# Delta rule's preparation: masks inside the clamp, products read from PSUM, two clamps on ScalarE

## The chip, the cores and the metric

One Trainium2 chip, one core. The metric is the device time of one execution in microseconds (us). Five engines work at once, each with its own queue in order: TensorE (PE, with its weight loads PEld), VectorE (DVE), ScalarE (ACT), GpSimd (POOL) and SyncE (SP), whose queue issues the DMAs here. SBUF is the on-chip memory, PSUM the memory that matrix products are written to.

## The reference

Two layers over 256 context tokens and 256 latent tokens, 1024 channels, in float32. A layer is a SwiGLU half step, a mix of three token mixers on one input, and another half step. The mixer that the change touches is the gated delta rule, 4 heads of 128 channels, forwards and backwards in time. Per chunk it solves a triangular system (cut; `incl` includes the diagonal, `strict` doesn't):

```
diff  = gc[..., :, None] - gc[..., None, :]
a_mat = einsum(kc, kc) * where(strict, exp(where(strict, diff, 0)), 0) * bc[..., :, None]
sol   = triangular_solve(eye(CHUNK) + a_mat, rhs, left_side=True, lower=True)
p_mat = einsum(qc, kc) * where(incl, exp(where(incl, diff, 0)), 0)
```

gc is the running sum of the log decays, bc the write strength. The other two mixers (retention, state-space) and the projections fill the time around it.

## The kernel before

All work is in float32; the large projections are made as three fast products each, so every weight block (128x512, one DMA of 256 KB, tile raw) is split into a high half by a cast on ScalarE (whi, L121) and a low half by a subtraction on VectorE or GpSimd (wlo, L123), and multiplied by L141, L142 and L143. Blocks are four buffers deep: a load waits until the casts have freed its buffer, a cast until TensorE has used the old half. 1313 such loads go through SyncE's queue, together with all other DMAs.

The function `gdn` computes the delta rule for a group of heads: heads 0 and 1, then 2 and 3 in layer 0; all four in layer 1. It projects and convolves (L533, L536), transposes (gtr), computes small columns (col), and then comes the preparation, L887 to L937, which the change is in. Chunks have 128 tokens here. For each pair of heads p, rows of running sums (Rg) and of strengths (Rb) are loaded as broadcasts; for each of four chunks c a body runs:

- L905: clamped differences on VectorE into six places of E: forward, two heads (min with 0), backward (min with 0; only where the chunk has output), and backward for the system (max with 0)
- L908, L909: exponentials on ScalarE, L909 with the sign turned
- L912, L915: products of keys with keys and with queries on TensorE, into one PSUM bank (kk, a pool of three banks, `mx`)
- L917: VectorE masks the first two into kks (strict upper triangle)
- L920, L921: the matrices M of both directions, from kks, a column and E
- L923: GpSimd multiplies M by the rows Rb
- L928: queries' products from PSUM times a column times a triangular mask into kq; L930: kq times E into PT (only where the chunk has output)
- `self.take(wt[2])`: TensorE gets other work to fill the time ("fill": projections and the retention mixer in `retention`, later the state-space projections)

In layer 0 all four chunks have output, in layer 1 only chunks 2 and 3. After the chunks L936 and L937 make Q from Rg and the queries.

Behind it SyncE's queue writes the diagonal 32x32 blocks of M to DRAM (d<-M, four writes), reads them back with another layout (B, L952), and VectorE substitutes in 31 steps (L957, L959, tiles tm and X). Then blocks are merged by products (tile XX) and the chunks are scanned.

The fill in these stretches includes the retention mixer (products rsc, L653; times a table into pt, L657 and L660, on VectorE; normalised output `on`, L680, and its transposes rof, L686) and the state-space mixer's projections (BC, transposes str, L1181; gates zs from products sz). The mixer itself has a clamp on ScalarE, L1281, followed by exponentials.

The framework orders each engine's queue at build time from priorities and estimated times, so the order in the queues isn't the order in the source.

Of the kernel before, what the change touches and what calls it, by code (L numbers as in the profile page):

```python
# [8 lines left out]
F32 = mybir.dt.float32  # L9
F32R = mybir.dt.float32r  # L10
I32 = mybir.dt.int32
AF = mybir.ActivationFunctionType
ALU = mybir.AluOpType
MUL, ADD, SUB, MAX, MIN = ALU.mult, ALU.add, ALU.subtract, ALU.max, ALU.min

P = 128
# [30 lines left out]
class Net:  # L47
# [410 lines left out]

    def mix_setup(self, ctx):
        nc, io, cp = self.nc, self.io, self.cp  # L460
        self.masks = cp.tile([P, 3, P], F32, name="masks")
        nc.sync.dma_start(out=self.masks, in_=io["masks"])
        self.triU, self.triL, self.triUs = (self.masks[:, i, :] for i in range(3))
        self.prow = cp.tile([P, DEPTH, PR_N], F32, name="prow")
        nc.sync.dma_start(out=self.prow, in_=io["prow"].rearrange("(o l) n -> o l n", o=1).broadcast_to([P, DEPTH, PR_N]))
        self.rt = cp.tile([P, 4, 48], F32, name="rt_")
        nc.gpsimd.memset(self.rt, 0.0)

        for lo, hi in ((PC_GCW, PC_GNG), (PC_GNG, PC_N)):
            v = self.pcol[:, :, lo:hi]  # L470
            nc.vector.tensor_scalar(out=v, in0=v, scalar1=0.5, scalar2=None, op0=MUL)
# [309 lines left out]
    def gdn(self, H, gp, pool0, gtok):  # L781
# [3 lines left out]
        nc, l, tc = self.nc, self.l, self.tc  # L785
        outs, och = self.outs, self.och
        nh, h0, n0 = len(H), H[0], och[0]
        nu, no = 2 * nh, len(och)
        wt = self.gdn_fill
        tag = f"{l}{h0}"  # L790
# [49 lines left out]
        for i, h in enumerate(H):  # L840
            ps = self.win_tile(OFF_GK + h * P, [0, 1], "gk")
# [3 lines left out]
            ps = self.win_tile(OFF_GQ + h * P, outs, "gq")  # L845
# [3 lines left out]
        for i, h in enumerate(H):  # L849
            ps = self.win_tile(OFF_GV + h * P, [0, 1], "gv")  # L850
# [13 lines left out]
        rk, rq, bb, w0, w1, nb0, nb1, tmp = (col[:, i] for i in range(8))  # L864
# [19 lines left out]
        M = gp.tile([P, 4, nu, P], F32, tag="M", name="M")  # L884
        PT = gp.tile([P, no, nu, P], F32, tag="PT", name="PT")
        Q = gp.tile([P, 2, nh, self.no], F32, tag="Q", name="Q")
        with ExitStack() as st:  # L887
            pp = st.enter_context(tc.tile_pool(name=f"gprep{tag}", bufs=1, side="right", reuse_waits="tile"))
            for p in range(0, nh, 2):
                Rg = pp.tile([P, 2, 2, T], F32, tag="Rg", name="Rg")  # L890
                Rb = pp.tile([P, 2, 2, T], F32, tag="Rb", name="Rb")
                for d in range(2):
                    self.rows_in(Rg[:, d], self.dR[d * 20 + h0 + p:d * 20 + h0 + p + 2, :])
                    self.rows_in(Rb[:, d], dB[d * nh + p:d * nh + p + 2, :])
                pair = lambda t, c: t[:, c].rearrange("p (d h) n -> p d h n", d=2)[:, :, p:p + 2]
                for c in range(4):
                    out = c in och
                    cs = ac(c)
                    E = pp.tile([P, 6, P], F32, tag="E", name="E", bufs=2)
                    for i in range(2):  # L900
                        for d, slot, op in ((0, i, MIN), (1, 2 + i, MIN), (1, 4 + i, MAX)):
                            if slot in (2, 3) and not out:
                                continue
                            g = h0 + p + i
                            nc.vector.tensor_scalar(out=E[:, slot], in0=Rg[:, d, i, cs], scalar1=self.G[:, c, d, g:g + 1],  # L905
                                                    scalar2=0.0, op0=SUB, op1=op)
                    ne = 4 if out else 2
                    nc.scalar.activation(out=fl(E[:, 0:ne]), in_=fl(E[:, 0:ne]), func=AF.Exp)  # L908
                    nc.scalar.activation(out=fl(E[:, 4:6]), in_=fl(E[:, 4:6]), func=AF.Exp, scale=-1.0)  # L909
                    ps = v4(self.mx("kk"))  # L910
                    for i in range(2):
                        nc.tensor.matmul(ps[:, i], kf[:, p + i, cs], kf[:, p + i, cs], start=True, stop=True)  # L912
                    if out:
                        for i in range(2):
                            nc.tensor.matmul(ps[:, 2 + i], kf[:, p + i, cs], qf[:, p + i, qc(c)], start=True, stop=True)  # L915
                    kks = pp.tile([P, 2, P], F32, tag="kks", name="kks", bufs=2)
                    nc.vector.tensor_tensor(out=kks, in0=ps[:, 0:2], in1=self.triUs.unsqueeze(1).to_broadcast([P, 2, P]), op=MUL)  # L917
                    for i in range(2):
                        q = p + i
                        nc.vector.scalar_tensor_tensor(out=M[:, c, q], in0=kks[:, i], scalar=rk[:, c, q:q + 1], in1=E[:, i], op0=MUL, op1=MUL)  # L920
                        nc.vector.scalar_tensor_tensor(out=M[:, c, nh + q], in0=kks[:, i], scalar=bb[:, c, q:q + 1], in1=E[:, 4 + i],  # L921
                                                       op0=MUL, op1=MUL)
                    nc.gpsimd.tensor_tensor(out=pair(M, c), in0=pair(M, c), in1=Rb[:, :, :, cs], op=MUL)  # L923
                    if out:
                        kq = pp.tile([P, 4, P], F32, tag="kq", name="kq", bufs=1)
                        for i in range(2):
                            for d, m in ((0, self.triU), (1, self.triL)):
                                nc.vector.scalar_tensor_tensor(out=kq[:, 2 * d + i], in0=ps[:, 2 + i], scalar=rk[:, c, p + i:p + i + 1],  # L928
                                                               in1=m, op0=MUL, op1=MUL)
                        nc.vector.tensor_tensor(out=pair(PT, c - n0), in0=kq.rearrange("p (d h) n -> p d h n", d=2),  # L930
                                                in1=E[:, 0:4].rearrange("p (d h) n -> p d h n", d=2), op=MUL)
                    self.take(wt[2])
                for d in range(2):
                    for i in range(2):
                        q_ = Q[:, d, p + i]
                        nc.scalar.activation(out=q_, in_=Rg[:, d, i, self.oc], func=AF.Exp)  # L936
                        nc.gpsimd.tensor_tensor(out=q_, in0=q_, in1=qf[:, p + i], op=MUL)  # L937
# [8 lines left out]
        with ExitStack() as st:  # L946
            pp = st.enter_context(tc.tile_pool(name=f"gsub{tag}", bufs=1, side="right", reuse_waits="tile"))
            n = 4 * nb
# [5 lines left out]
            for s in range(31):  # L954
# [3 lines left out]
                                        in1=X[:, s, 0:b].unsqueeze(1).to_broadcast([n, a, b]), op=MUL)  # L958
# [23 lines left out]
        with ExitStack() as st:  # L982
            pp = st.enter_context(tc.tile_pool(name=f"gmrg{tag}", bufs=1, side="right", reuse_waits="tile"))
# [738 lines left out]
def constants():  # L1722

    i, j = np.arange(P)[:, None], np.arange(P)[None, :]
    m = np.zeros((P, 3, P), np.float32)
    m[:, 0] = i <= j
    m[:, 1] = i >= j
    m[:, 2] = i < j
    d = np.arange(384)[None, :] - P - np.arange(P)[:, None]
    dist = d.astype(np.float32)  # L1730
    n_freq = P // 4
    inv = (np.float32(10000.0) ** (-np.arange(n_freq, dtype=np.float32) / np.float32(n_freq))).astype(np.float32)
    tok = np.arange(NS)
    ang = np.concatenate([(tok // 64).astype(np.float32)[:, None] * inv, (tok % 64).astype(np.float32)[:, None] * inv], -1).T
    cos, sin = np.cos(ang).astype(np.float32), np.sin(ang).astype(np.float32)
    rope = np.stack([np.concatenate([cos, cos]), np.concatenate([-sin, sin])], 1)
    return {"ident": np.eye(P, dtype=np.float32), "masks": m, "dist": dist, "rope": np.ascontiguousarray(rope),
            "eye32": np.eye(32, dtype=np.float32)}
# [65 lines left out]
```

## Time and profile before

| | |
|---|---|
| median of 3 runs | 2776.03 us (2774.65 to 2779.43) |
| the profiled execution | 2773.71 us, of which the span 2771.9 us |
| TensorE busy | 94% of the span |
| VectorE busy | 75% |
| ScalarE busy | 44% |
| GpSimd busy | 27% |
| granted clock of TensorE, mean | 0.978 of full speed |

Busy time is that of instructions in work. A matmul's end is modelled, so a busy TensorE need not be at its peak. A wait names the instruction that was released last.

### The profile page before, as it was taken

Reading aid. Unit: us, or ns where it says so; the run is one execution under the profiler, and the core shown is the slowest. Engines: PE = TensorE matmul, PEld = TensorE weight load, DVE = VectorE, ACT = ScalarE, POOL = GpSimd, SP = SyncE. Lnnn points to the kernel's source line nnn. Section 1 sums busy time; section 2 is a strip of 40 time slices with the busy share of each in tenths; the row PEclk is TensorE's granted clock in tenths of the full one; section 3 lists DMA queues with packets and bytes.
Section 4 is the critical chain, followed back from the end, with each engine's and each line's share of the span. In section 5 each row is a group of like instructions: output and inputs, shape, how many; then the busy total and the mean of one; then the engine's idle time right before and its main releaser. Section 6 shows DMA issues by size and latency. Waiting matters only on the chain.

```text
span 2771.9 us, 45529 instructions
## 1 busy us (share of the span) xinstructions
PE 2602.5 (94%) x16136; PEld 2216.4 (80%) x16136; DVE 2088.3 (75%) x4122; ACT 1213.0 (44%) x2388; POOL 745.7 (27%) x627
## 2 busy tenths in 40 slices
PE   8999999899899999999999999999988889889998
PEld 6888887777777777888887888888877768778997
DVE  5888878868878585488987778854778885786666
ACT  3333256344345643363332543323655354554553
POOL 1000144422444454250000520002443433453100
PEclk9999999999999999999999999999999999999999
DMA  8566655423425455366665466643545333656665
GB/s 280 178 187 188 172 165 147 118 62 105 147 77 158 155 152 156 106 172 197 194 187 185 136 208 195 189 125 97 174 115 166 110 99 89 194 184 187 199 183 152
DMA packets 292808, 435.99 MB, mean 157 GB/s; under 512 B 42628, under 2 KB 109828, under 8 KB 292452
## 3 DMA queue, kind: packets, MB, share of 16 engines
q1 hardware_dynamic: 292580, 433.09, 53.1%
q8 instruction: 126, 2.06, 0.3%
q14 instruction: 102, 0.84, 0.1%
HBM read 401.86 MB, written 31.13 MB: 156 GB/s over the span
## 4 chain that ended last, share of the span: by engine, by line
PE 63%; DVE 19%; DMA 7%; issue 5%; ACT 3%; POOL 3%; SPq 1%; DVEq 0%; ACTq 0%; POOLq 0%
PE p L141 9%; PE p L143 9%; PE p L142 9%; DVE cacc L533 4%; DMA raw<-wst 4%; PE pd L141 3%; PE pd L143 3%; PE pd L142 3%; DVE wlo L123 3%; PE gate L141 1%; PE gate L143 1%; PE gate L142 1%; ACT whi L121 1%; PE br L141 1%; PE br L143 1%
## 5 line engine op out<-in xcount | busy, mean ns | idle before, releaser
L121 ACT CAST whi<-raw 128x512 fp32r<-128x512 f32 x1003 | 613.5, 617 | 819.5 <-PE pd L142 195.4
L123 DVE TENSOR_TENSOR wlo<-raw,whi 128x512 fp32r<-128x512 f32 x803 | 596.8, 746 | 233.3 <-ACT whi L121 226.5
L141 PE MATMUL p<-uh,whi 128*128 128x512 f32 (+1 forms) x1216 | 445.3, 366 | 1.8 <-ACT whi L121 1.8
L143 PE MATMUL p<-uh,wlo 128*128 128x512 f32 (+1 forms) x1216 | 440.2, 362 | 0.2 <-DVE wlo L123 0.2
L142 PE MATMUL p<-ul,whi 128*128 128x512 f32 (+1 forms) x1216 | 440.2, 362 | 0.0
L123 POOL TENSOR_TENSOR wlo<-raw,whi 128x512 fp32r<-128x512 f32 x200 | 288.5, 1445 | 484.5 <-ACT whi L121 467.6
L190 DVE SCALAR_TENSOR_TENSOR acc<-raw,cT,acc 128x512 f32<-128x512 f32 x448 | 320.5, 753 | 87.9 <-DMA raw<-wst 86.2
L307 POOL TENSOR_TENSOR y<-y,piv 128x256 f32<-128x256 f32 x30 | 27.6, 950 | 884.5 <-ACT piv L305 884.5
L141 PEld LDWEIGHTS p<-uh,whi 128*128 128x128 f32 x1216 | 229.0, 188 | 43.4 <-ACT whi L121 4.4
L143 PEld LDWEIGHTS p<-uh,wlo 128*128 128x128 f32 x1216 | 229.1, 188 | 37.3 <-DVE wlo L123 0.6
L142 PEld LDWEIGHTS p<-ul,whi 128*128 128x128 f32 x1216 | 229.2, 188 | 34.2
L141 PE MATMUL pd<-ach,whi 128*128 128x512 f32 (+1 forms) x660 | 232.0, 351 | 0.0
L143 PE MATMUL pd<-ach,wlo 128*128 128x512 f32 (+1 forms) x660 | 229.4, 348 | 0.0
L142 PE MATMUL pd<-acl,whi 128*128 128x512 f32 (+1 forms) x660 | 229.2, 347 | 0.0
L533 DVE SCALAR_TENSOR_TENSOR cacc<-craw,pcol,cacc 128x508 f32<-128x508 f32 (+2 forms) x192 | 169.4, 889 | 17.6 <-ACT cacc L528 16.0
L141 PEld LDWEIGHTS pd<-ach,whi 128*128 128x128 f32 x660 | 125.0, 189 | 17.4 <-ACT whi L121 1.4
L143 PEld LDWEIGHTS pd<-ach,wlo 128*128 128x128 f32 x660 | 125.0, 189 | 16.3 <-DVE wlo L123 0.5
L142 PEld LDWEIGHTS pd<-acl,whi 128*128 128x128 f32 x660 | 125.0, 189 | 15.2
L141 PE MATMUL gate<-uh,whi 128*128 128x512 f32 (+1 forms) x384 | 135.4, 353 | 0.0
L143 PE MATMUL gate<-uh,wlo 128*128 128x512 f32 (+1 forms) x384 | 130.9, 341 | 0.8 <-POOL wlo L123 0.8
L142 PE MATMUL gate<-ul,whi 128*128 128x512 f32 (+1 forms) x384 | 131.4, 342 | 0.0
L411 ACT CAST ach<-pr 128x512 fp32r<-128x512 f32 (+1 forms) x88 | 50.0, 568 | 164.8 <-DVE pr L410 164.8
(477 smaller groups left out, 6057.4 us busy)
## 6 DMA issues: line engine op xcount, KB each, us to landing
raw<-wst SPq DMA_DIRECT2D x1313, 256.0 KB, 2.8
R<-dR SPq DMA_DIRECT2D x24, 512.0 KB, 6.0
dah<-y SPq DMA_DIRECT2D x9, 1024.0 KB, 5.6
y<-dah SPq DMA_DIRECT2D x28, 256.0 KB, 5.1
Rg<-dR SPq DMA_DIRECT2D x8, 512.0 KB, 5.2
Rb<-dB SPq DMA_DIRECT2D x8, 512.0 KB, 4.6
dx<-xo SPq DMA_DIRECT2D x16, 256.0 KB, 2.9
xt<-dx SPq DMA_DIRECT2D x4, 1024.0 KB, 8.4
```

The costliest lines, as they stand in the source:

```text
L121: nc.scalar.copy(out=hi, in_=r)
L123: e.tensor_tensor(out=lo, in0=r, in1=hi.bitcast(F32), op=SUB)
L141: nc.tensor.matmul(out, wh, xh, start=start, stop=False)
L142: nc.tensor.matmul(out, wh, xl, start=False, stop=False)
L143: nc.tensor.matmul(out, wl, xh, start=False, stop=stop)
L190: eng.scalar_tensor_tensor(out=acc, in0=r, scalar=c, in1=acc, op0=MUL, op1=ADD)
L307: (nc.gpsimd if m >= self.ln_dve[0] else nc.vector).tensor_tensor(out=y[:, m, c], in0=y[:, m, c], in1=piv, op=SUB)
L411: nc.scalar.copy(out=F["ach"][:, m], in_=pr[:, :n])
L533: nc.vector.scalar_tensor_tensor(out=a[:, :, lo:hi], in0=r[:, :, lo + d:hi + d], scalar=w[:, tap:tap + 1], in1=a[:, :, lo:hi], op0=MUL, op ...
```

## The change

The mask tile gets four parts instead of three: the two triangles with their diagonals, and two with 0 inside the triangle and -30000 outside. The clamp of the forward and backward places becomes one instruction that subtracts and takes the minimum with such a mask, so that the exponential is 0 outside the triangle. The third clamp (backward, for the system) goes to ScalarE as Relu with a negated column as bias; the negated columns nG are made once per pair of heads. M and PT are computed straight from the products in PSUM; kks and kq and their instructions go. M's lower triangle and diagonal, which nothing reads, are no longer zeroed.

```
-        self.masks = cp.tile([P, 3, P], F32, name="masks")
+        self.masks = cp.tile([P, 4, P], F32, name="masks")
-        self.triU, self.triL, self.triUs = (self.masks[:, i, :] for i in range(3))
+        self.triU, self.triL, self.minU, self.minL = (self.masks[:, i, :] for i in range(4))
...
+                nG = pp.tile([P, 4, 2], F32, tag="nG", name="nG", bufs=2)
+                nc.vector.tensor_scalar(out=nG, in0=self.G[:, :, 1, h0 + p:h0 + p + 2], scalar1=-1.0, scalar2=None, op0=MUL)
...
                     for i in range(2):
-                        for d, slot, op in ((0, i, MIN), (1, 2 + i, MIN), (1, 4 + i, MAX)):
-                            if slot in (2, 3) and not out:
-                                continue
-                            g = h0 + p + i
-                            nc.vector.tensor_scalar(out=E[:, slot], in0=Rg[:, d, i, cs], scalar1=self.G[:, c, d, g:g + 1],
-                                                    scalar2=0.0, op0=SUB, op1=op)
+                        g = h0 + p + i
+                        for d, low in ((0, self.minU), (1, self.minL)):
+                            if d == 0 or out:
+                                nc.vector.scalar_tensor_tensor(out=E[:, 2 * d + i], in0=Rg[:, d, i, cs], scalar=self.G[:, c, d, g:g + 1],
+                                                               in1=low, op0=SUB, op1=MIN)
+                        nc.scalar.activation(out=E[:, 4 + i], in_=Rg[:, 1, i, cs], func=AF.Relu, bias=nG[:, c, i:i + 1])
...
-                    kks = pp.tile([P, 2, P], F32, tag="kks", name="kks", bufs=2)
-                    nc.vector.tensor_tensor(out=kks, in0=ps[:, 0:2], in1=self.triUs.unsqueeze(1).to_broadcast([P, 2, P]), op=MUL)
...
-                        nc.vector.scalar_tensor_tensor(out=M[:, c, q], in0=kks[:, i], scalar=rk[:, c, q:q + 1], in1=E[:, i], op0=MUL, op1=MUL)
-                        nc.vector.scalar_tensor_tensor(out=M[:, c, nh + q], in0=kks[:, i], scalar=bb[:, c, q:q + 1], in1=E[:, 4 + i],
+                        nc.vector.scalar_tensor_tensor(out=M[:, c, q], in0=ps[:, i], scalar=rk[:, c, q:q + 1], in1=E[:, i], op0=MUL, op1=MUL)
+                        nc.vector.scalar_tensor_tensor(out=M[:, c, nh + q], in0=ps[:, i], scalar=bb[:, c, q:q + 1], in1=E[:, 4 + i],
                                                        op0=MUL, op1=MUL)
...
-                        kq = pp.tile([P, 4, P], F32, tag="kq", name="kq", bufs=1)
                         for i in range(2):
-                            for d, m in ((0, self.triU), (1, self.triL)):
-                                nc.vector.scalar_tensor_tensor(out=kq[:, 2 * d + i], in0=ps[:, 2 + i], scalar=rk[:, c, p + i:p + i + 1],
-                                                               in1=m, op0=MUL, op1=MUL)
-                        nc.vector.tensor_tensor(out=pair(PT, c - n0), in0=kq.rearrange("p (d h) n -> p d h n", d=2),
-                                                in1=E[:, 0:4].rearrange("p (d h) n -> p d h n", d=2), op=MUL)
+                            for d in range(2):
+                                nc.vector.scalar_tensor_tensor(out=PT[:, c - n0, d * nh + p + i], in0=ps[:, 2 + i], scalar=rk[:, c, p + i:p + i + 1],
+                                                               in1=E[:, 2 * d + i], op0=MUL, op1=MUL)
...
-    m[:, 2] = i < j
+    m[:, 2:] = (m[:, :2] - 1) * np.float32(30000.0)
```

## Rows read from the trace of the kernel before

**Rows 1.** The page: busy us, share of the span and instructions of each engine.

```profile
PE 2602.5 (94%) x16136; PEld 2216.4 (80%) x16136; DVE 2088.3 (75%) x4122; ACT 1213.0 (44%) x2388; POOL 745.7 (27%) x627
```

**Rows 2.** Windows, three preparations: length, busy PE, PEld, DVE, ACT, POOL; clock, DMA.

```profile
487.00:532.00 45.00, 43.35 (x202) 34.88 (x201) 36.17 (x79) 19.16 (x39) 25.87 (x24) 1.00 0.58 155
690.00:736.00 46.00, 44.74 (x211) 37.11 (x210) 36.14 (x82) 19.65 (x37) 26.67 (x23) 1.00 0.64 181
2103.00:2173.00 70.00, 57.72 (x349) 50.11 (x347) 68.53 (x182) 33.55 (x75) 30.83 (x26) 0.95 0.48 152
```

**Rows 3.** Waits of PE, 480 to 545: total us, times, longest.

```profile
PE rsc L653 <- DVE pt L657: 6.7, 1, 6.7
...
PE rg L143 <- DVE wlo L123: 1.5, 1, 1.5
```

**Rows 4.** Waits of PE, 685 to 760.

```profile
PE str L1181 <- DVE BC L536: 7.0, 1, 7.0
PE sz L143 <- POOL wlo L123: 1.3, 1, 1.3
```

**Rows 5.** Waits of PE, 2096 to 2175.

```profile
PE rsc L653 <- DVE pt L660: 5.2, 3, 4.0
PE rof L686 <- DVE on L680: 4.7, 2, 2.5
PE rq L141 <- ACT whi L121: 1.2, 1, 1.2
```

**Rows 6.** Groups of DVE, whole span: count | busy us, mean ns | idle before.

```profile
L905 DVE TENSOR_SCALAR E<-Rg,G 128x128 f32<-128x128 f32 x88 | 33.2, 426 | 5.2 <-DMA Rg<-dR 5.2
L920 DVE SCALAR_TENSOR_TENSOR M<-kks,col,E 128x128 f32<-128x128 f32 x32 | 17.1, 543 | 0.1
L921 DVE SCALAR_TENSOR_TENSOR M<-kks,col,E 128x128 f32<-128x128 f32 x32 | 15.3, 488 | 0.0
L928 DVE SCALAR_TENSOR_TENSOR kq<-kk,col,masks 128x128 f32<-128x128 f32 x48 | 14.2, 339 | 0.0
L930 DVE TENSOR_TENSOR PT<-kq,E 128x512 f32<-128x512 f32 x12 | 13.2, 1098 | 0.0
L917 DVE TENSOR_TENSOR kks<-kk,masks 128x256 f32<-128x256 f32 x16 | 6.6, 414 | 0.7 <-PE kk L915 0.7
```

**Rows 7.** Instructions by tile (E; kq): count: ns shortest/median/longest, first and last start.

```profile
L1281 ACT ACTIVATE E<-R,G x192: 383/388/405, 872.8 to 2479.1; 128x128 f32<-128x128 f32 x192
L905 DVE TENSOR_SCALAR E<-Rg,G x88: 271/277/1382, 488.2 to 2166.2; 128x128 f32<-128x128 f32 x88
L920 DVE SCALAR_TENSOR_TENSOR M<-kks,col,E x32: 335/346/1397, 496.7 to 2168.5; 128x128 f32<-128x128 f32 x32
L930 DVE TENSOR_TENSOR PT<-kq,E x12: 677/684/1796, 499.8 to 2170.8; 128x512 f32<-128x512 f32 x12
L928 DVE SCALAR_TENSOR_TENSOR kq<-kk,col,masks x48: 331/339/347, 489.7 to 2170.2; 128x128 f32<-128x128 f32 x48
```

**Rows 8.** Timeline of DVE: start, us, instruction.

```profile
702.36 1.37 DVE L920 SCALAR_TENSOR_TENSOR M<-kks,col,E 128x128 f32<-128x128 f32 x1
...
707.54 1.11 DVE L928 SCALAR_TENSOR_TENSOR kq<-kk,col,masks 128x128 f32<-128x128 f32 x4
```

**Rows 9.** Timeline of POOL; in brackets the idle time before and its releaser.

```profile
701.83 3.04 POOL L937 TENSOR_TENSOR Q<-Q,qf 128x512 f32<-128x512 f32 x2 [2.24 <-ACT Q L936]
```

**Rows 10.** Waits of ACT, 480 to 545.

```profile
ACT E L908 <- DVE E L905: 14.6, 4, 4.5
```

**Rows 11.** Products kk of PE, 480 to 530.

```profile
L912 PE MATMUL kk<-kf x16: 270/275/275, 486.8 to 505.6; 128*128 128x128 f32 x16
```

**Rows 12.** Timeline of SyncE's queue, 476 to 545.

```profile
518.31 0.34 SPq L945 DMA_DIRECT2D d<-M  x1
...
523.75 0.34 SPq L110 DMA_DIRECT2D raw<-wst  x1
524.14 0.42 SPq L945 DMA_DIRECT2D d<-M  x1
```

More of the change, by code (lines that the diff above doesn't have):

```diff
@@ L1724, in constants @@
     i, j = np.arange(P)[:, None], np.arange(P)[None, :]
-    m = np.zeros((P, 3, P), np.float32)
+    m = np.zeros((P, 4, P), np.float32)
     m[:, 0] = i <= j
     m[:, 1] = i >= j
-    m[:, 2] = i < j
+    m[:, 2:] = (m[:, :2] - 1) * np.float32(30000.0)
     d = np.arange(384)[None, :] - P - np.arange(P)[:, None]
```

## The prediction

> **What bounds the kernel now.** First the busy shares of the whole execution: TensorE is busy for 94% of 2771.9 us, VectorE for 75%, ScalarE for 44%, GpSimd for 27% [rows 1]. TensorE's work doesn't change here, apart from waits. So the question is how much of its idle time hangs on the delta rule's preparation.
>
> The preparation runs three times: heads 0 and 1 of layer 0, heads 2 and 3 of layer 0, all four heads of layer 1. I cut one window per run, from the first product of keys to the start of the substitution or the last PT [rows 2]. In the first two, TensorE is busy for 43.35 of 45 and 44.74 of 46 us while VectorE has 36 us of work; in the third VectorE is busy for 68.53 of 70 us and TensorE for only 57.72. There VectorE is the bound, and TensorE's 12.3 idle us are the price.
>
> Then who holds TensorE up, in windows stretched to the waits that the preparation causes further on. Layer 0, first run: 6.7 us in one piece for the retention table product (the tile pt) behind VectorE's queue, and 1.5 us for a weight's low half on VectorE [rows 3]. Second run: 7.0 us for BC and 1.3 us for a low half on GpSimd [rows 4]. Layer 1: 5.2 us for pt and 4.7 us for the normalised retention output on VectorE, besides 1.2 us for a weight cast [rows 5]. The ceiling of what these stages can give back is 8.2 + 8.3 + 12.3 = 28.8 us.
>
> **The change part by part.** There are 16 bodies (a pair of heads, one chunk of 128 tokens): 12 with output, 4 without (chunks 0 and 1 of layer 1, two pairs).
>
> *VectorE before.* 88 clamps, 16 maskings into kks, 64 products for M, 48 for kq and 12 for PT: 228 instructions, 99.6 us by the six groups [rows 6]. Two things are in that sum. One is plain length: 0.277 us a clamp, 0.346 a product from SBUF, 0.339 a product from PSUM, 0.684 a PT [rows 7], 0.414 a kks [rows 6]. In a row they start closer than they last: four kq products take 1.11 us together [rows 8], so they start (1.11 - 0.34) / 3 = 0.26 us apart, and each instruction occupies the engine for about 0.08 us less than its length. The other is stalls: M products that read two SBUF tensors take 1.37 us, four times in a row from 702.36 on [rows 8], while GpSimd works on Q without a break [rows 9]. Clamps and PT show it too (maxima 1.38 and 1.80), but the 48 products that read PSUM and a mask never do: 331 to 347 ns [rows 7]. So on this trace a VectorE instruction is held up by GpSimd when it reads two SBUF tensors or is a clamp, and not when one operand is in PSUM.
>
> By starts, mean lengths times counts less 0.08 us each: 37.5 + 6.6 + 17.4 + 15.6 + 16.3 + 13.2 - 228 x 0.08 = 88 us occupied. Without stalls it would be 88 x 0.20 + 16 x 0.33 + 64 x 0.26 + 48 x 0.26 + 12 x 0.60 = 59 us.
>
> *VectorE after.* 56 clamps with a mask (4 in each of 12 bodies, 2 in each of 4), 64 M products from PSUM, 48 PT products from PSUM: 168 instructions at 0.26 = 44 us. The clamps now read Rg and a mask, two SBUF tensors, so I give them the mean stall of the old M products: (17.4 + 15.6) / 64 - 0.346 = 0.17 us, times 56 = 9.5 us. M and PT get none, after kq. The four small instructions for nG I take as whole clamps, 1 us. Sum 54.5 us, so 33 to 34 us less VectorE time; 34 below. Bounds: 14 us, if every stall moves to a neighbour (59 - 45), and 43 us, if the clamps escape it (88 - 45). I take 34, as the trace has both kinds of product side by side.
>
> [...]
>
> *ScalarE.* 32 clamps move there as Relu with a column as bias. The state-space stage runs exactly that form at 0.388 us [rows 7]: 12.4 us. ScalarE is busy for 19.16 of 45, 19.65 of 46 and 33.55 of 70 us [rows 2], so about 0.8 us more in each body finds room. What covers it is idleness in front of the exponentials: in the first run they wait 14.6 us for VectorE's clamps [rows 10], and those now have fewer ahead of them. Queued behind a Relu are the weight casts that TensorE lives on; if the cover were gone, the 12.4 us would be the price. No exchange of function tables is charged: Relu and Exp already alternate there.
>
> *Removed tiles, and a wait.* kks and kq go. The product's bank is now read only after the exponential, so it is held longer. The pool has three such banks, and TensorE's next products queue behind a held one. In the first run the products are issued from 486.8 to 505.6 us [rows 11], some 6 us apart, so a bank has three such steps to come free. I charge nothing; without that slack it would be up to one 6 us step per run. M's diagonal and lower part are no longer zeroed; nobody's instruction count hangs on it. The mask load grows from 192 to 256 KB and is made once, early, on a queue of 1313 weight loads of that size: nothing.
>
> *What reaches the end.* GpSimd finishes M, SyncE's queue writes its diagonal blocks to DRAM and reads them back, and VectorE substitutes. In the first run the queue hangs at the first write until 518.31; the fourth leaves at 524.14, behind a weight load at 523.75 [rows 12], and the read back later still. Weight loads wait until casts free their buffers, and those follow TensorE. So an M that is ready 10 us earlier does not move the read back by 10 us: once the queue is no longer held up by M, it is held by weights. I take the 1.5 us for the low half and 1 us of the 6.7: **2.5 us**, between 0 and 8.2. In the second run GpSimd, not weights, trails M, so I take 3 of the 7.0 us and 1 of the 1.3: **4 us**, between 0 and 8.3. In layer 1 the queue in front of pt and the retention output loses its share of the 34 us (100 of 228 instructions, 15 us of 68.5), which should pay about half of TensorE's idle time: **6 us**, between 0 and 12.3. Sum 12.5 us. What is late next is the weight stream and, after the substitution, DMA; neither is touched.
>
> **The rivals.**
> 1. *The queue gives nothing away.* The preparation gets faster, but the read back stays behind weight loads, and the time is lost as a longer wait for DRAM. For it: the weight load ahead of the last write [rows 12]. Against it: layer 1's waits for pt and on are in the same VectorE queue, with no DRAM between. Then 0 to 5 us come back: 2771 to 2776.
> 2. *The whole ceiling.* The order of the queues, which is chosen at build time, moves with the shorter preparation, and nearly all 28.8 us return. For it: all long waits name VectorE. Against it: the queue of [rows 12]. Some 20 to 29 us: 2747 to 2756.
> 3. *Slower: ScalarE blocks the weights.* A Relu must wait for the row load and for E's buffer (two of them, freed by VectorE), and the casts behind it on ScalarE stand. TensorE pays as now at a late cast, 1.2 us [rows 5], once a body: 16 x 1.2 = 19, less the 12.5 gained: 7 us slower, 2783. It decides once a Relu stands longer than the casts are ahead; today's waits of the exponentials, 14.6 us over four bodies, some 4 us each [rows 10], cost TensorE nothing in that run.
>
> **How the numbers follow.** The profiled execution took 2773.71 us (span 2771.9); 2773.7 - 12.5 = 2761.2. The median of the runs shown is 2776.03, 2.3 us more, so 2763.5. Chances: forecast, 6 to 20 us gained, 0.48; rival 1 (within 5.5 us of the old time) 0.23; rival 2, 0.14; rival 3 and any other loss, 0.15. A measurement of this kernel can tell about 0.2%, 5.5 us, from no change. So faster 0.62, same 0.23, slower 0.15. The range leaves out the best of rival 2 and the worse part of rival 3: 2749 to 2779; the forecast's own is 2756 to 2770.
>
> **What would show it right or wrong.** In the profile after: M and PT products reading PSUM at 0.34 us with no maximum above 0.4; masked clamps near 0.35 with maxima near 1.4; 32 more Relu at 0.39; the groups of [rows 6] shrunk from 99.6 to some 65 us busy (168 x 0.34 + 9.5); TensorE's waits for pt and on in layer 1 about halved; the 6.7 us of [rows 3] hardly shorter. Wrong would be: M products slow from PSUM, waits of TensorE for weight casts in these windows, or TensorE standing at a product kk.

## The result and the profile after

Seven runs of the changed kernel have a median of 2762.19 us (2758.49 to 2771.60), seven of the kernel before beside them 2777.51 us (2767.07 to 2786.65): ratio 0.9949, interval [0.9929, 0.9970], some 14 us faster; 12.5 us were forecast. The profiled execution took 2766.53 us (span 2764.7). The seven executions of one kernel spread over 13 us (changed) and 20 us (before), so gains below are read in the stages, not from two spans.

Groups of VectorE after; columns as in [rows 6]:

```profile
L907 DVE SCALAR_TENSOR_TENSOR E<-Rg,G,masks 128x128 f32<-128x128 f32 x56 | 39.5, 751 | 2.4 <-DMA Rg<-dR 2.4
L929 DVE SCALAR_TENSOR_TENSOR PT<-kk,col,E 128x128 f32<-128x128 f32 x48 | 13.5, 340 | 0.0
L922 DVE SCALAR_TENSOR_TENSOR M<-kk,col,E 128x128 f32<-128x128 f32 x32 | 10.9, 342 | 2.7 <-ACT E L911 2.0 <-PE kk L918 0.7
L923 DVE SCALAR_TENSOR_TENSOR M<-kk,col,E 128x128 f32<-128x128 f32 x32 | 10.9, 341 | 1.9 <-ACT E L912 1.9
L897 DVE TENSOR_SCALAR nG<-G 128x8 f32<-128x8 f32 x4 | 1.6, 429 | 0.0
```

The 228 instructions of 99.6 us became 172 of 76.4 us, not of 65. The M and PT products that read PSUM run at their plain length, 0.340 to 0.342 us on average; the masked clamps take 0.751 us on average, where 0.346 + 0.17 = 0.516 was assumed. By tile (columns as in [rows 7]):

```profile
L907 DVE SCALAR_TENSOR_TENSOR E<-Rg,G,masks x56: 314/418/1459, 490.1 to 2154.1; 128x128 f32<-128x128 f32 x56
L929 DVE SCALAR_TENSOR_TENSOR PT<-kk,col,E x48: 335/341/345, 499.5 to 2159.6; 128x128 f32<-128x128 f32 x48
L909 ACT ACTIVATE E<-Rg,nG x32: 385/389/402, 497.2 to 2139.3; 128x128 f32<-128x128 f32 x32
L922 DVE SCALAR_TENSOR_TENSOR M<-kk,col,E x32: 335/342/351, 498.4 to 2156.5; 128x128 f32<-128x128 f32 x32
```

The timelines say why. VectorE, layer 0, first run:

```profile
505.26 6.84 DVE L907 SCALAR_TENSOR_TENSOR E<-Rg,G,masks 128x128 f32<-128x128 f32 x6
512.03 0.34 DVE L922 SCALAR_TENSOR_TENSOR M<-kk,col,E 128x128 f32<-128x128 f32 x1
```

and GpSimd over the same time:

```profile
505.32 2.74 POOL L936 TENSOR_TENSOR Q<-Q,qf 128x512 f32<-128x512 f32 x2
508.02 1.35 POOL L925 TENSOR_TENSOR M<-M,Rb 128x512 f32<-128x512 f32 x1
509.32 2.63 POOL L123 TENSOR_TENSOR wlo<-raw,whi 128x512 fp32r<-128x512 f32 x2
```

Six clamps take 6.84 us while GpSimd puts five instructions of 1.3 to 1.4 us end to end: about one clamp gets in per GpSimd instruction. The masked clamps are the only VectorE instructions of the preparation left that read two SBUF tensors. By means less medians the six groups of before held 29 us of stalls (13 of clamps, 11 of M, 5 of PT, [rows 6] and [rows 7]); the masked clamps alone now hold some 23: most of what M and PT lost went to them. In the same run four masked clamps from 495.72 on, with GpSimd idle from 495.65 to 497.36, take 1.14 us together; the six above take 1.14 us each on average, beside GpSimd's 1.3 to 1.4 us, and the longest of all 56 is 1.459 us.

Waits of TensorE in the windows of [rows 3] and [rows 4], and around layer 1's preparation (2087 to 2164, [rows 5]):

```profile
PE rsc L654 <- DVE pt L658: 4.1, 1, 4.1
...
PE str L1180 <- DVE BC L537: 6.2, 1, 6.2
...
PE rof L687 <- DVE on L681: 5.0, 2, 2.6
PE rsc L654 <- DVE pt L661: 2.9, 1, 2.9
PE rq L143 <- POOL wlo L123: 1.6, 1, 1.6
```

In layer 0 both waits for a low half are gone and the long ones are 2.6 and 0.8 us shorter (1.6 and 1.4 in e0_after, the changed kernel built again). In layer 1 the waits for pt and on make 7.9 us instead of 9.9 (10.8 in e0_after): not halved.

Stage lengths worked out from the traces of all kernels told of below (us). "to M" runs from the first load of Rg to the end of the last GpSimd product of M, "to gXT" to the first transposition behind the substitution. X to gXT: from the substitution's end in the second run of layer 0. "Stretch": the same 450 projection products from the 2850th to the 3300th (790 to 965 us before); "next": the 450 after them.

```
                   layer 0 first   layer 0 second  layer 1         X to   stretch  next
                   to M   to gXT   to M   to gXT   to M   to gXT   gXT
before             36.4    97.3    34.8   108.5    73.0   168.9    11.6   174.7   143.9
after              33.4    92.9    30.2   104.3    71.5   168.6    10.9   172.1   141.7
e0_after           32.6    92.1    30.2   103.1    72.5   171.1    10.9   171.1   141.7
e2_no_relu         29.8    89.5    31.7   105.8    68.9   164.4    11.2   172.7   140.1
c1_dead            34.8    94.4    30.8   103.3    71.4   170.3    11.1   172.8   139.6
g1_write_first     33.0    92.1    30.8   104.8    69.4   149.6    10.9   172.2   141.0
d1_more_early      36.5    96.5    34.4   113.5    74.2   167.9    10.7   178.4   141.2
e1_relu_alone      34.5    95.9    34.6   119.4    72.7   169.9    20.0   187.4   141.5
e3_clamps_on_act   31.0    91.0    31.8   111.9    66.3   162.7    15.4   187.5   142.2
c3_m_only          34.7    96.6    35.5   118.1    67.1   163.2    16.0   187.8   142.5
h1_lo_vector       29.9    90.6    28.0   110.7    72.1   170.8    18.5   187.3   139.6
f1_fill4_after     32.4    93.3    30.9   111.6    64.2   148.4    18.1   181.5   141.4
f2_fill4_before    34.8    97.5    36.6   122.5    69.2   151.3    20.2   189.4   139.6
```

To gXT, the change gains 4.4 us (5.2 in e0_after) in the first run, 4.2 (5.4) in the second and nothing in layer 1. These columns count whatever else TensorE was given in between, and that differs between builds: in the first run 314 projection products before and 305 after, in layer 1 some 610 in both, but 519, 483 and 487 in g1, f1 and f2, whose 20 us less to gXT are therefore no gain. All kernels run the same series of 11388 projection products (a few dozen near the 9300th change places in g1, f1 and f2). Between the same two products, the changed kernel gains 1.8 us in the first run (1980th to 2400th; 5.2 in e0_after), 3.9 (5.1) in the second and the merging behind it (to the 3100th), 4.2 (5.2) from there to the 3750th, and in layer 1 (8300th to 9900th) it loses 2.2 (gains 0.3).

Another 5 us (4.8 and 5.8) come in layer 0's state-space mixer, where nothing was changed ("stretch" 2.6 and 3.6, "next" 2.2). One piece of that shows. VectorE's chain of small instructions for snv, before the change:

```profile
973.98 1.25 DVE L258 TENSOR_TENSOR snv<-snv 128x1 f32<-128x1 f32 x1
975.26 0.16 DVE L259 SCALAR_TENSOR_TENSOR snv<-snv 128x1 f32<-128x1 f32 x1
975.46 2.32 DVE L260 SCALAR_TENSOR_TENSOR snv<-snv 128x1 f32<-128x1 f32 x1
```

against a GpSimd instruction that had just begun:

```profile
973.94 1.27 POOL L123 TENSOR_TENSOR wlo<-raw,whi 128x512 fp32r<-128x512 f32 x1 [3.96 <-ACT whi L121]
975.42 2.34 POOL L1288 TENSOR_TENSOR R<-R,BC 128x1024 f32<-128x1024 f32 x1 [0.21 <-ACT R L1287]
```

and the same chain after, whose last instruction begins 0.04 us ahead of that low half (969.72):

```profile
969.30 0.15 DVE L258 TENSOR_TENSOR snv<-snv 128x1 f32<-128x1 f32 x1
969.49 0.16 DVE L259 SCALAR_TENSOR_TENSOR snv<-snv 128x1 f32<-128x1 f32 x1
969.68 0.16 DVE L260 SCALAR_TENSOR_TENSOR snv<-snv 128x1 f32<-128x1 f32 x1
```

TensorE's waits for snv, before (962 to 1060) and after (957 to 1053; 7.4 us in e0_after):

```profile
PE sv L1330 <- DVE snv L260: 11.2, 2, 6.3
...
PE sv L1329 <- DVE snv L260: 7.6, 2, 4.6
```

Which of two instructions started first, by hundredths of a microsecond, decided 3.3 us of VectorE's time here (3.73 us in these three instructions before, 0.47 after); no step of the change aims at it.

### The profile page after: what moved, and what is told of

Its sections match the earlier page's. It is cut to its first block, busy times and chain, and to the rows that moved or that the text cites. A ratio compares the mean times of both kernels' runs of the same rounds, so it can differ in the third digit from the quotient of the medians.

```text
span 2764.7 us, 45511 instructions
## 1 busy us (share of the span) xinstructions
PE 2611.5 (94%) x16136; PEld 2227.3 (81%) x16136; DVE 2068.5 (75%) x4066; ACT 1222.5 (44%) x2420; POOL 749.7 (27%) x627
## 5 line engine op out<-in xcount | busy, mean ns | idle before, releaser
L534 DVE SCALAR_TENSOR_TENSOR cacc<-craw,pcol,cacc 128x508 f32<-128x508 f32 (+2 forms) x192 | 169.1, 886 | 17.8 <-ACT cacc L529 16.2
```

What stands on the lines that cost most here:

```text
L534: nc.vector.scalar_tensor_tensor(out=a[:, :, lo:hi], in0=r[:, :, lo + d:hi + d], scalar=w[:, tap:tap + 1], in1=a[:, :, lo:hi], op0=MUL, op ...
```

## The experiments

Three theories stood against each other, and a fourth, P, was added later. V: VectorE's time in the preparation is what pays. S: ScalarE's queue pays or costs. O: the order of the queues, chosen anew at each build, pays by chance; P: TensorE's other work, put between two chunks, sets the pace. The first four ran together (before: 2774.20 us, 11 runs), the rest beside 28 and 35 runs of the kernel before. A difference to the changed kernel is that of the two ratios times 2775 us.

**e0_after**, the changed kernel again.

> The changed kernel itself, beside the others of this call. Theory V (VectorE's time in the preparation is what pays): some 14 us, 0.5%, faster than before, as in the result. Rival O (the queues' order, newly chosen at build time, pays by chance, and the saved VectorE time little): the same, since the program is the same.

2759.3 us, ratio 0.9947 [0.9931, 0.9963]: the result stands.

**e1_relu_alone**, the kernel before with only the third clamp moved to ScalarE.

```
-  for d, slot, op in ((0, i, MIN), (1, 2 + i, MIN), (1, 4 + i, MAX)):
+  for d, slot, op in ((0, i, MIN), (1, 2 + i, MIN)):
...
+  nc.scalar.activation(out=E[:, 4 + i], in_=Rg[:, 1, i, cs], func=AF.Relu, bias=nG[:, c, i:i + 1])
```

> Only the third clamp moves to ScalarE; masks, kks and kq stay as before. VectorE loses 32 of its 88 clamps, 32 x 0.38 = 12 us of the group's 33.2 us busy; ScalarE gains 32 x 0.39 = 12 us. V: 12 of 34 us saved, so about a third of the gain, 4 to 5 us (0.17%) faster than before. O: no relation to the VectorE time; anywhere from 8 us slower to 8 us faster.

2789.45 us, 1.0051 [1.0037, 1.0065]: 14 us slower than before. The table says where: the way to M is 1.9 and 0.2 us shorter, not longer, and the stretch behind is 12.7 us longer. So the loss isn't in the preparation, where the Relus are (see "The read back of X" below).

**e2_no_relu**, the changed kernel with that clamp left on VectorE.

```
-  nc.scalar.activation(out=E[:, 4 + i], in_=Rg[:, 1, i, cs], func=AF.Relu, bias=nG[:, c, i:i + 1])
+  nc.vector.tensor_scalar(out=E[:, 4 + i], in0=Rg[:, 1, i, cs], scalar1=self.G[:, c, 1, g:g + 1], scalar2=0.0, op0=SUB, op1=MAX)
```

> The change without its ScalarE part: the third clamp stays on VectorE, masks in the clamp and products from PSUM as changed. V: the other two thirds of the gain, 9 to 10 us (0.35%) faster than before, 4 to 5 us slower than the changed kernel. O: no order among the three; this one could be the fastest.

2759.35 us, 0.9943 [0.9926, 0.9960]: the same as the changed kernel. Moving 32 clamps to ScalarE brings nothing clear of noise. It relieves VectorE by 4 us only: here 56 masked clamps take 30.2 us (568 ns each) and 32 plain ones 13.7, together 43.9, where the changed kernel's 56 alone take 39.5.

**e3_clamps_on_act**, all clamps on ScalarE, the triangle multiplied onto the products in PSUM.

```
-  nc.vector.scalar_tensor_tensor(out=E[:, 2 * d + i], in0=Rg[:, d, i, cs], ..., in1=low, op0=SUB, op1=MIN)
+  nc.scalar.activation(out=E[:, i], in_=Rg[:, 0, i, cs], func=AF.Relu, scale=-1.0, bias=self.G[:, c, 0, g:g + 1])
...
+  for d, m in ((1, self.triL), (0, self.triU)):
+      kq = ps[:, 2 - 2 * d:4 - 2 * d]
+      nc.vector.tensor_tensor(out=kq, in0=ps[:, 2:4], in1=m.unsqueeze(1).to_broadcast([P, 2, P]), op=MUL)
```

> All six clamps of a body go to ScalarE as Relu, and the triangular masks of PT are put on the products inside PSUM (two instructions a body with output, never two SBUF tensors). VectorE loses 56 masked clamps, which stand at 0.751 us each with stalls (39.5 us busy), and gains 24 maskings of some 0.41 us (10 us): 30 us less than in the changed kernel. ScalarE gains 56 x 0.31 = 17 us. V: about as much again as the change, 10 to 13 us faster than the changed kernel (0.9% faster than before). O: within 8 us of the changed kernel. A third reading, S: ScalarE's queue, with the weight casts behind the clamps, becomes what TensorE waits for, and the kernel is slower than the changed one by up to 17 us.

2763.89 us, 0.9963 [0.9949, 0.9978]: 4.4 us slower than the changed kernel, with overlapping intervals and 28 us less on VectorE (48.3 against 76.4 us). The way to M is 2.4 us shorter than after, 1.6 longer and 5.2 shorter, and the stretch behind, again, takes 15 us more; that loss hides what less VectorE time would have been worth.

**d1_more_early and d2_more_last**, the changed kernel with 48 extra products on VectorE, spread over chunks 0 to 2 or all in chunk 3.

```
+  for n in range(4 if c < 3 else 0):        # d2: range(12 if c == 3 else 0)
+      w = pp.tile([P, P], F32, tag="more", name="more", bufs=2)
+      nc.vector.scalar_tensor_tensor(out=w, in0=ps[:, n % 2], scalar=rk[:, c, p:p + 1], in1=E[:, n % 2], op0=MUL, op1=MUL)
```

> The changed kernel with extra work on VectorE that is no part of the computation: in chunks 0, 1 and 2 of every pair, four products of the keys' product in PSUM with E into a scratch tile, ahead of those for M. 48 products at some 0.26 us are 12.5 us more in all, 3.1 us per pair. Theory P (pace: TensorE's fill sets when each chunk's products come, and VectorE's time only counts as the lag from the last product of keys to M's end): work in the early chunks is caught up before the last one, so the lag stays at 7.5 to 8.5 us in all three preparations and the kernel stays within 3 us of the changed one. Theory V (VectorE's time in the preparation pays wherever it lies, some 12 us for 30 to 34 us saved): 12.5 x 0.4 = 5 us slower. Theory O (the order of the queues chosen at build time): no relation to the 12.5 us, up to 8 us either way.

> The changed kernel with the same 48 extra products, all in the last chunk of each pair (12 each, 3.1 us), ahead of those for M; again no part of the computation. Theory P: the lag from the last product of keys to M's end grows by 3 us in each preparation, from 7.5 to 8.5 to some 11, near the 10 to 12 us of the kernel before, and the kernel is 6 to 9 us slower than the changed one. Theory V: 5 us slower, the same as with the work in the early chunks. Theory O: no relation, up to 8 us either way.

d1: 2766.12 us, 0.9972 [0.9959, 0.9984], 6.9 us slower than the changed kernel (V said 5, P up to 3). In layer 0 the 3.1 us per run make M 3.1 to 4.2 us later, back at the times of before (36.5 and 34.4 against 36.4 and 34.8), so there work ahead of M in VectorE's queue still sets M's end. That speaks against P in layer 0; in layer 1 too the lag that P expected to stay grows, from 7.7 to 14.0 us. But M's end alone doesn't set TensorE's time. The substitution begins only 1.3 to 2.1 us later than in the changed kernel, as from M's end to it 11.5 and 11.2 us pass instead of 13 to 14; and between the same products d1 still gains about 6 us on the kernel before in the first run, and 0.9 in the second.

d2: 2776.81 us, 1.0008 [0.9992, 1.0024]: the whole gain lost, 17 us, more than any theory said. Its trace, of an execution of 3621.66 us at a mean granted clock of 0.652, gives no times to compare; how much of the 17 us is M and how much is order stays open.

**f1_fill4_after and f2_fill4_before**, less of TensorE's other work between two chunks and more behind, in the changed kernel and in the one before.

```
-  self.gdn_fill = ((2, 4, 5, 18, 1, 1, 3, 4), (2, 4, 5, 20, 0.5, 0.35, 3, 4))[self.outs[0]]
+  self.gdn_fill = ((2, 4, 4, 22, 1, 1, 3, 4), (2, 4, 4, 28, 0.5, 0.35, 3, 4))[self.outs[0]]
```

> The changed kernel with TensorE's other work that is put between two chunks of the preparation cut from 5 to 4 us a body, and that behind it raised from 18 to 22 us (layer 0) and from 20 to 28 us (layer 1). Theory P: the spread from the first to the last product of keys shrinks by some 4 us in both runs of layer 0 (from 19.5 and 20) and by up to 8 us in layer 1 (from 64); M's end comes as much earlier, since VectorE now keeps up, and the kernel is 0 to 8 us faster than the changed one. If VectorE, not the fill, sets the pace, the spread stays and nothing is gained. Theory O: up to 8 us either way with the spread as it is.

> The kernel before with the same cut of the work between the chunks, from 5 to 4 us a body. Theory P: here VectorE has no room to follow, so that the spread from the first to the last product of keys shrinks but the lag to M's end (12, 12 and 10 us) grows by as much, and the kernel stays within 4 us of the kernel before, less gained than by the same cut in the changed kernel. If TensorE's fill alone set the pace, it would gain as much as the changed kernel does. Theory O: up to 8 us either way.

f1: 2781.94 us, 1.0020 [1.0006, 1.0035]; f2: 2799.48 us, 1.0096 [1.0078, 1.0114]: 20 and 27 us slower than the kernels they were made from, so as a tuning both miss. For the cause they are useful. In layer 0 f1's M ends as before the cut (32.4 and 30.9 against 33.4 and 30.2): not the fill but VectorE and GpSimd set that pace. The spread from the first to the last product of keys did shrink, by 3.2 and 3.4 us, and the lag behind it grew from 7.7 and 7.6 to 9.4 and 11.7. In layer 1 M ends 7.3 us earlier (64.2 against 71.5), as P says; the kernel before, with more on VectorE, gains 3.8 us there from the same cut. But with the old fill that time lies anywhere from 66.3 (e3) to 74.2 (d1), and c3, with more on VectorE, has 67.1: the fill is one part of the pace, the order of the queues another. Nor did the earlier M pay: between the same products of layer 1 (8300th to 9900th) f1 and f2 lose 10.7 and 16.5 us to the kernel before. In f1, TensorE also stands 2.9 us at a product kk until VectorE has made M, the wait for a held bank that the prediction charged at nothing; in the changed kernel no such wait appears.

**c1_dead**, an instruction per pair that nobody reads, as a control of the order.

```
+  dead = pp.tile([P, 4, 2], F32, tag="dead", name="dead", bufs=2)
+  nc.vector.tensor_scalar(out=dead, in0=nG, scalar1=-1.0, scalar2=None, op0=MUL)
```

> Control for the order of the queues: the changed kernel with one extra small VectorE instruction per pair of heads (128x8, 0.43 us, four in all, 1.7 us) whose result nobody reads; not part of the computation. Theory O (the order chosen at build time pays or costs by chance): the order shifts around it and the time moves by several us either way, up to 8. Theory V (VectorE's occupied time in the preparation is what counts): unchanged within 1 us.

2764.25 us, 0.9965 [0.9950, 0.9980]: 5 us slower than the changed kernel for 1.7 us of work, with an interval that overlaps that of e0_after. Its stages are those of the changed kernel but for 1.4 to 2.2 us more to the first M. Differences of 5 us between two builds aren't to be read as the worth of an edit.

**c3_m_only**, the changed kernel with PT by way of kq as before.

```
-  nc.vector.scalar_tensor_tensor(out=PT[:, c - n0, d * nh + p + i], in0=ps[:, 2 + i], ..., in1=E[:, 2 * d + i], ...)
+  nc.vector.scalar_tensor_tensor(out=kq[:, 2 * d + i], in0=ps[:, 2 + i], ..., in1=m, op0=MUL, op1=MUL)
...
+  nc.vector.tensor_tensor(out=pair(PT, c - n0), in0=kq..., in1=E[:, 0:4]..., op=MUL)
```

> Half of the change: masked clamps, Relu on ScalarE and M straight from PSUM, but PT again by way of kq (its masks then do nothing new). It puts back 48 products at 0.26 us less the 48 that read PSUM, and 12 of the long PT products, 7 us by starts plus their stalls (5 us in the kernel before): 7 to 12 us of VectorE's 34. Theory V: 0.4 x 7 to 12, 3 to 5 us slower than the changed kernel, and the wait for M grows, as PT's products lie in front of the next chunk's M. If only the path to M counts and PT is free: within 2 us of the changed kernel. Theory O: no relation.

2780.14 us, 1.0012 [0.9996, 1.0029]: 18 us slower than the changed kernel, where V said 3 to 5. M comes 1.3 and 5.3 us later in layer 0, and 15.7 us more lie in the stretch behind.

**g1_write_first**, M's writes and the read back ahead of the weight loads.

```
+  with tc.high_priority():
       nc.sync.dma_start(out=d1[b].rearrange("u r c -> r u c"), in_=Mu[...])
...
+  with tc.high_priority():
       nc.sync.dma_start(out=B, in_=d1.rearrange("b u r c -> (b u) r c"))
```

> The changed kernel, with the four writes of M's diagonal blocks and the read back put ahead of the weight loads between them in SyncE's queue. It tests the step that the read back is held by weight loads once M is no longer late. If that is so: from M's end to the read back 7.9, 9.1 and 18.2 us shrink to 3 to 5 us each, the substitution begins 4 us (layer 0) to 10 us (layer 1) earlier, and the kernel gains 3 to 8 us over the changed one. If the distance shrinks and the time stays, the read back wasn't what TensorE waited for. If the distance stays, it is the transfers' own time.

2770.93 us, 0.9980 [0.9963, 0.9997]: 9 us slower than the changed kernel. From M's end the last write leaves after 2.0, 1.5 and 5.7 us (e0_after: 5.3, 5.7, 12.0) and the read back after 7.0, 5.9 and 16.4 (7.9, 9.1, 18.1), and still the substitution begins hardly earlier in layer 0 and later in layer 1: 13.0, 13.0 and 25.6 us against 13.3, 13.3 and 23.5. VectorE's waits in the second run and in layer 1 name what came instead:

```profile
DVE zs L546 <- DMA dz<-zs: 3.6, 1, 3.6
...
DVE tm L958 <- DMA X<-eye: 1.3, 1, 1.3
...
DVE on L681 <- DMA dy<-yo: 8.5, 1, 8.5
```

The start value of X, which I hadn't moved, is now the last to land, and VectorE waits for other transfers too. Between the same products g1 loses 5.4 us to the kernel before in layer 1, where e0_after gains 0.3.

**h1_lo_vector**, every second low half of layer 0's preparation on VectorE instead of GpSimd.

```
-  plo = self.plo = ((3, 4, 2, 2, 3, 2), (4, 1, 3, 4, 2, 2))[l]
+  plo = self.plo = ((3, 2, 2, 2, 3, 2), (4, 1, 3, 4, 2, 2))[l]
```

> The changed kernel, with every second low half of a weight moved from GpSimd to VectorE during layer 0's two preparations (there GpSimd made all of them). GpSimd is then busy for less, and VectorE has some 10 us of room per preparation. If GpSimd is the late one since the change (it trails M, and its instructions hold the masked clamps, 0.75 us each against 0.32): masked clamps of layer 0 fall to some 0.5 us, M's end comes 1 to 3 us earlier in both, and the kernel gains 2 to 6 us. If VectorE's own time counts (theory V): some 15 low halves at 0.6 us on VectorE cost 9 us of its time, 0.4 x 9 = 3 to 4 us slower.

2773.93 us, 0.9986 [0.9971, 1.0002]: 11 us slower than the changed kernel. Its local claim holds. Masked clamps of the first run, 482 to 520, in e0_after:

```profile
L907 DVE SCALAR_TENSOR_TENSOR E<-Rg,G,masks 128x128 f32<-128x128 f32 x16 | 13.6, 905 | 2.0 <-DMA Rg<-dR 2.0
```

and in h1_lo_vector:

```profile
L907 DVE SCALAR_TENSOR_TENSOR E<-Rg,G,masks 128x128 f32<-128x128 f32 x16 | 7.2, 504 | 0.0
```

M ends 2.7 and 2.2 us earlier than in e0_after, with more work on VectorE, as it should if GpSimd's hold on the clamps costs there. GpSimd made 3 low halves in the first run's preparation instead of 6, VectorE 4 instead of 2. Their number isn't all: in d1, with 7 on GpSimd, the clamps took 9.3 us, so when the clamps fall counts too. Then the stretch behind takes 16.2 us more, and the kernel loses.

**The read back of X.** A loss of 9 to 16 us in the stretch, each against the kernel it was made from, stands in e1, e3, c3, h1, f1 and f2 (f1 and f2 also moved work into it), none in before, after, e0, e2, c1 and g1. The column beside it tells them apart: from the substitution's end to gXT 15 to 20 us instead of 11. (d1's 178.4 is another loss: its gXT is on time.) The order of SyncE's queue tells them apart as well, and it is the build's, not one execution's: the last load of X stands behind 390 weight loads in before, after, e0, e2, c1 and g1, behind 391 in f1, 392 in e1, e3, c3, h1 and f2, and 394 in d1 and d2. SyncE's queue there, e0_after:

```profile
773.97 0.47 SPq L960 DMA_DIRECT2D d<-X  x1
774.93 0.39 SPq L1187 DMA_DIRECT2D dx<-xo  x1
777.69 0.33 SPq L110 DMA_DIRECT2D raw<-wst  x1
778.06 1.42 SPq L1047 DMA_DIRECT2D XX<-d  x3
781.66 0.35 SPq L110 DMA_DIRECT2D raw<-wst  x1
```

and h1_lo_vector:

```profile
780.08 0.50 SPq L1047 DMA_DIRECT2D XX<-d  x1
781.79 0.33 SPq L110 DMA_DIRECT2D raw<-wst  x1
782.16 0.93 SPq L1047 DMA_DIRECT2D XX<-d  x2
790.70 0.35 SPq L110 DMA_DIRECT2D raw<-wst  x1
791.10 1.91 SPq L1047 DMA_DIRECT2D XX<-d  x4
```

Three of X's eight loads leave before the second weight load in the one, one in the other; and the third weight load stands until 790.70, with the last five loads of X behind it; 7.5 us of that, by the queue's waits, are for a low half on GpSimd. TensorE pays, in h1 (772 to 797):

```profile
PE gXT L998 <- DMA XX<-d: 5.6, 1, 5.6
```

The windows of the 25 us around it (columns as in [rows 2]), e0_after and then h1:

```profile
776.00:801.00 25.00, 24.55 (x313) 19.23 (x313) 16.38 (x27) 15.40 (x36) 8.89 (x12) 0.97 0.38 89
```

```profile
772.00:797.00 25.00, 18.16 (x89) 13.86 (x88) 13.88 (x20) 9.71 (x18) 11.50 (x11) 0.84 0.40 106
```

TensorE is busy for 6.4 us less, and the granted clock of these 25 us is 0.84 instead of 0.97. The whole stretch, e0_after and then h1:

```profile
780.54:951.68 171.14, 162.71 (x1167) 131.42 (x1166) 121.89 (x219) 97.49 (x211) 70.99 (x48) 0.99 0.48 134
```

```profile
776.86:964.17 187.31, 168.93 (x1170) 135.80 (x1169) 119.66 (x220) 97.71 (x213) 75.73 (x56) 0.95 0.42 124
```

Of the 16.2 us, 10 are idle time of TensorE, 5.6 of it the wait at gXT, and 6.2 are longer busy time for nearly the same count of instructions, at a granted clock of 0.95 instead of 0.99. That the order of these loads costs it is read from the traces; a kernel in which only that order is changed was not run.

Sorted by that order, the change shows all the same. With X's last load behind 390 weight loads the ratios are 1 before and 0.9943 to 0.9980 for the kernels with the change in whole or part; behind 391 or 392 they are 1.0051 (e1) and 1.0096 (f2) for those that keep the old products, and 0.9963 to 1.0020 for e3, h1, c3 and f1; behind 394 there are only d1 and d2, 0.9972 and 1.0008. f1 and f2 are before and after once more, with another fill: f1 is the faster by 0.76%, 17.5 us of the medians. So the gain is hardly an accident of one order, though order moves single builds by as much.

## Why the prediction was right, and where its sum was not

- **Total.** 12.5 us forecast, 14 us measured, ratio 0.9949 [0.9929, 0.9970]. Neither the unchanged (rival 1) nor the 20 to 29 us (rival 2) came. But the terms compensate each other: that the sum came so close is partly luck.
- **VectorE's time.** Less 0.08 us each, 76.4 - 172 x 0.08 = 62.6 us remain, so 25 us were saved, not 34. "I give them the mean stall of the old M products", 0.17 us, was the mis-sized term: measured (0.751 - 0.346) = 0.405 us each, 23 us instead of 9.5. The stalls weren't saved with the instructions that had them; part went to the neighbours, as the lower bound allowed.
- **PSUM as source.** Right: 335 to 352 ns for M and PT with no outlier, 341 on average against 346 from SBUF, and in a row they start 0.26 us apart either way.
- **Layer 0, first run.** 2.5 us forecast; 4.4 and 5.2 measured to gXT, 1.8 and 5.2 between the same products. That M's lead would be lost in SyncE's queue was wrong for the change: M ends 3.0 to 3.8 us earlier, and the substitution starts 4.9 to 5.5 us earlier after the first load of Rg (46.5 and 45.9 us against 51.4). **Second run:** 4 forecast; 4.2 and 5.4 measured to gXT, 3.9 and 5.1 between the same products. d1 undoes the lead of M in both with 3.1 us of VectorE work, so M's lead does come from VectorE's queue. But the start of the substitution then moves back by less than M, as the queue step said, and TensorE's gain in the first run stays. That TensorE gains through M is not shown; the rows show its waits for pt, BC and low halves shrink.
- **Layer 1.** "Should pay about half of TensorE's idle time: 6 us" failed: 0.3 us in the profiled run, -2.2 in e0_after. VectorE's busy time fell from 68.53 of 70 us to 60.1 of 70 (2091 to 2161), by 8.4 us where 15 were forecast, yet TensorE was busy for 60.35 of 70, as idle as VectorE. The step took a busy share of 98% for the bound. Between the same products layer 1 gives -2.2 and 0.3 us. f1 points to TensorE's own other work between the chunks as a part of M's pace; what else sets it there is not settled.
- **Layer 0's mixer.** 5 to 6 us that no step foresaw; GpSimd's hold on the snv chain is one part, the rest is open.
- **ScalarE (rival 3).** The Relus take 389 ns, as told, and ScalarE loads a function table five times in each kernel, 1.283 us each: no more with the Relus than without. No wait of TensorE for a weight cast appeared in these windows, and e2 shows that they give nothing either. That e1 is slower than before fits rival 3's sign, not its mechanism: the loss is at X's read back.

No version beat the changed kernel: e2 equals it, and h1 has the shortest way to M in layer 0; what it would be worth with X's loads in their old place was not run.

## What to carry to other kernels

Before pricing an instruction with two SBUF inputs at its own length, look in the trace at what GpSimd does beside it: here the old M products took 1.37 us instead of 0.34 four times in a row, beside GpSimd instructions of 1.29 to 1.52, and of the 16 us of stalls that M and PT lost some 10 came back in the masked clamps. The 112 products with an operand in PSUM escaped it here (335 to 352 ns). A high busy share names the bound only if the consumer's idle time ends on it: put work back (d1) or move the other engine's (f1) before pricing a share. Where queues are ordered anew at each build, look for the one transfer whose place differs before crediting or blaming an edit; here the kernels with X's loads further back lost 9 to 16 us in one stretch, as much as the whole change gained. And compare builds between the same products of a fixed series: the time to a landmark counts work that the build moved across it.

## What was not expected of the hardware

- VectorE's 128x1 instructions of 0.16 us, which move next to nothing, took 1.25 and 2.32 us, as long as the GpSimd instructions (1.27 and 2.34 us) that had begun 0.04 us before them.
- More work on VectorE can shorten the stalls: in d1 the masked clamps of the first run took 9.3 us instead of 13.6, beside 3.4 us of extra products from PSUM; in h1 7.2 us, with twice the low halves on VectorE.
